# Dividing the third attention's products instead of its weights, an earlier spread of the inverses, and three of eight squares summed on GpSimd

## Chip, cores and metric

One NeuronCore of a Trainium2 chip runs the whole kernel. The metric is the device time of one execution in microseconds; three runs of the kernel before took 2602.8, 2603.32 and 2605.36, median 2603.32.

## What is computed

Two transformer blocks, run one after the other on a batch of one with 512 positions and a width of 1024. The first has a sparse attention with an index (layer A), a perceptron, an attention with a forgetting gate (layer B), a second perceptron and a last norm; the second has a grouped-query attention with norms and rotations of queries and keys (layer C here), a perceptron, a gated unit (gMLP) and a last perceptron, with modulation from a condition vector. What the change touches, of the reference:

```python
def rms_norm(x, g):
    x32 = x.astype(jnp.float32)
    y = x32 * lax.rsqrt(jnp.mean(x32 * x32, axis=-1, keepdims=True) + EPS)
    return (y * g.astype(jnp.float32)).astype(x.dtype)
...
    def one_block(q_blk):
        s = jnp.einsum('bqkgd,bskd->bkgqs', q_blk, k).astype(jnp.float32) * scale
        p = jax.nn.softmax(s, axis=-1).astype(v.dtype)
        return jnp.einsum('bkgqs,bskd->bqkgd', p, v)
```

The sum of squares of a norm runs over the width; the softmax of a head divides each row of weights by its sum, and dividing the product with v by the same sum gives the same result.

## The kernel before

Activations lie feature-major in eight tiles `h[k]` of 128x512 float32 (128 features by 512 positions). Precision comes from splitting each operand into a high and a low part (`split`, `weight`: high by a copy on ACT, low by a subtraction on DVE or GpSimd, names ending in h and l), and each product is three matmuls (`mul3`: high by high, low by high, high by low).

All instructions are recorded first and ordered afterwards by the program's own scheduler (`Sched`, from L155). `record` notes dependences and gives an instruction its place in the program as priority, plus what `later(n)` adds; `order` plays the engines with a table of costs and takes, on each engine that is free, the ready instruction of the lowest number whose output tile can be had; `emit` writes that order out. So all instructions carry the line L414. A tile of a name (tag) can be had when the earlier tiles of that tag have been begun, in their order, and one of its buffers is free. The eight PSUM banks are a pool with four tags: mm, lg and tp may have three each, po two, and all share four beyond the first of each. A bank of po is what heads' products, the sum of squares and the spreads use.

`squares` (L583) sums the squares of the eight `h[k]`: ACT squares into tiles "sq" (one buffer) and "y" in turn, DVE adds into `acc`, and four matmuls with ones sum over the features. `rms` (L601) makes the inverse root of it, and `spread` lays it out over all partitions by four transposes into a po bank and an ACT copy y. `rms` runs four times: at the start of layer A, ahead of the first perceptron, at the start of layer B, and ahead of the second perceptron.

`heads` (L813) treats a pair of heads. For each, `softmax` makes logits (lg), takes the masked row minimum (pr, mn, one DVE instruction each for the four blocks), exponentiates on ACT with the row sum beside it, and, unless `late` is set, makes a reciprocal (rs, 128x1) on DVE and scales pr by it on GpSimd. `turned` then transposes pr (tp), splits it into th and tl, and PE multiplies by v into a po bank; ACT copies one half (top) and DVE adds the other into `both` (o). With `late`, the sums of both heads are inverted together: `inverses` makes one reciprocal of 128x8, a wide copy on ACT (its tile is also called top, with one buffer) and four transposes into a po bank, and DVE multiplies `both` by that. Layer A calls `heads` with `late` 16 times (eight over half the positions, with the `narrow` form, eight over the other half); layer B and layer C call it eight times each without.

`layer_c` (L1066) also holds the first block's last norm: `spread(x.r)` and eight multiplications of `h` by its result (h<-h,vec,y) are recorded ahead of the attention under `later(2000)`, so that they give way to it. Then come the eight pairs, whose queries are projected, normed and rotated two pairs ahead (q, rot, sqh, msh, rh).

Of the kernel before, what the change touches and what calls it, by code (L numbers as in the profile page):

```python
# [14 lines left out]
ALU = mybir.AluOpType  # L15
# [3 lines left out]
P = 128  # L19
S = 512  # L20
# [3 lines left out]
NB = S // P  # L24
# [466 lines left out]
class Net:  # L491
# [91 lines left out]
    def squares(self, col=None):  # L583

        nc = self.nc
        acc = self.t(self.np_, "acc", [P, S])
        for k in range(KD):
            kw = {} if col is None else {"scale": self.vec[:, col + k : col + k + 1]}
            sq = acc if k == 0 else self.t(self.np_, "sq", [P, S], bufs=1) if k % 2 else self.t(self.np_, "y", [P, S])
            nc.scalar.activation(sq, self.h[k], AF.Square, **kw)  # L590
            if k:
                nc.vector.tensor_tensor(acc, acc, sq, ALU.add)
        ps = self.po()
        for b in range(NB):
            nc.tensor.matmul(ps[:, 2 * b : 2 * b + 2], acc[:, b * P : (b + 1) * P], self.ones[:, 0:2], start=True, stop=True)
        return ps[:, 0 : 2 * NB : 2]
# [216 lines left out]
    def heads(self, pool, npr, nth, lhs, rhs, v, o, masks=None, causal=True, rows=(None, None), blocks=range(NB), narrow=False, late=False):  # L813


        nc = self.nc
        n = len(blocks) * P
        W = {i: (i + 1) * P if causal else S for i in blocks}
        keys = range(max(W.values()) // P)
        sums = self.t(pool, "sums", [P, 2 * len(blocks)])  # L820
        both = self.t(pool, "o", [P, n], bufs=1)
        for h in range(2):
            pr = self.softmax(pool, npr, lhs[h], rhs[h], W, masks, rows[h], sums, h, late)
            po = self.po()
            for b in keys:
                th, tl, c = self.turned(pool, nth, pr, W, b)
                if narrow:
                    for x, (part, y) in enumerate(((0, th), (0, tl), (64, th))):
                        nc.tensor.matmul(po[0:64, c], v[h][b][:, part : part + 64], y[:, c], start=b == 0 and x == 0, stop=b == keys[-1] and x == 2)
                else:  # L830
                    nc.tensor.matmul(po[:, c], v[h][b], th[:, c], start=b == 0, stop=False)
                    nc.tensor.matmul(po[:, c], v[h][b], tl[:, c], start=False, stop=b == keys[-1])
            r = slice(64 * h, 64 * h + 64)
            if narrow:
                nc.scalar.activation(both[r], po[0:64, :n], AF.Copy)
            else:
                top = self.t(pool, "top", [P, n], bufs=1)[0:64]
                nc.scalar.activation(top, po[0:64, :n], AF.Copy)
                nc.vector.tensor_tensor(both[r], po[64:128, :n], top, ALU.add)
        if late:  # L840
            nc.vector.tensor_tensor(both, self.inverses(pool, sums, len(blocks)), both, ALU.mult)
        self.split(o[0][:, :n], o[1][:, :n], both)

    def attn_out(self, o, w, gate=None, norm=None):
# [221 lines left out]
    def layer_c(self, x, gate, norm):  # L1066
        nc, I, tc = self.nc, self.I, self.tc
        xh, xl = x.xh, x.xl
        *kps, q0 = self.first([I["w_k_c"][0], I["w_k_c"][1], I["w_q_c"][0]], xh, xl)
        with self.sched.after(), self.sched.later(2000):  # L1070
            rb = self.spread(x.r)
            for k in range(KD):
                g = self.vec[:, V_GF + k : V_GF + k + 1]
                nc.vector.scalar_tensor_tensor(self.h[k], self.h[k], g, rb, ALU.mult, ALU.mult)
        with ExitStack() as c1:
            pool = c1.enter_context(tc.tile_pool(name="c", bufs=2))
            tab = {}
            for w, col in (("q", V_QG), ("k", V_KG)):
                for m in range(2):
                    a = self.t(pool, f"tab{w}{m}", [P, S], bufs=1)  # L1080
                    nc.sync.dma_start(a, I["rope_c"][m])
                    nc.gpsimd.tensor_scalar(a, a, self.vec[:, col + m : col + m + 1], 1.0, ALU.mult, ALU.mult)
                    tab[w, m] = a
            v = [self.t(pool, f"v{b}", [P, 4, P], F32R, 1) for b in range(NB)]
            bd = self.t(pool, "bd", [P, 2], bufs=1)
            zero = self.t(pool, "zero", [P, S], bufs=1)
            nc.gpsimd.memset(zero, 0.0)
            nc.gpsimd.memset(bd, 0.0)
            nc.gpsimd.memset(bd[0:64, 0:1], 1.0)
            nc.gpsimd.memset(bd[64:128, 1:2], 1.0)  # L1090

            def inverse(ps, st):

                sq = self.t(pool, "sqh", [P, S], bufs=1)
                nc.scalar.activation(sq, ps, AF.Square)
                for b in range(NB):
                    nc.tensor.matmul(st[:, 2 * b : 2 * b + 2], sq[:, b * P : (b + 1) * P], bd, start=True, stop=True)
                ms = self.t(pool, "msh", [P, 8])
                nc.vector.tensor_scalar(ms, st[:, 0:8], 1.0 / HD, EPS, ALU.mult, ALU.add)
                rr = self.t(pool, "rh", [P, 8], bufs=4)  # L1100
                nc.gpsimd.tensor_tensor(rr, ms, self.mhalf, ALU.pow)
                return rr

            def evac_v(b, ps):
                x = ps.rearrange("p (n d) -> p n d", n=4)
                self.split(v[b][:, :, 0:64], v[b][:, :, 64:128], x)

            kd = []
            self.tm(I["w_v_c"], xh, xl, evac_v, ("po", "po", "lg", "tp"))
            for ps in kps:  # L1110
                s = self.rope(pool, ps, tab["k", 0], tab["k", 1], nc.gpsimd)
                st = self.lg()
                rr = inverse(ps, st)
                wide = self.t(pool, "o", [P, S], bufs=1)
                nc.scalar.activation(wide.rearrange("p (a d) -> p a d", a=8), rr.rearrange("p (a o) -> p a o", o=1).to_broadcast([P, 8, HD]), AF.Copy)
                for b in range(NB):
                    nc.tensor.transpose(st[:, b * P : (b + 1) * P], wide[:, b * P : (b + 1) * P], self.ident)
                nc.vector.tensor_tensor(s, st, s, ALU.mult)
                kd += self.doubles(pool, "kd", s, -0.125)
            qs, o = [], []  # L1120
            for j in range(KD + 2):
                if j < KD:
                    with self.sched.later(200 if j > 1 else 0):
                        self.low = nc.gpsimd if j > 2 else None
                        ps = q0 if j == 0 else self.fm(I["w_q_c"][j], xh, xl)
                        self.low = None
                        s = self.rope(pool, ps, tab["q", 0], tab["q", 1], nc.gpsimd if j else nc.vector)
                        rr = inverse(ps, ps)
                        qs.append((self.stacks(pool, "st", s, 16), rr))
                if j < 2:  # L1130
                    continue
                j -= 2
                st, rr = qs[j]
                n = j // 2
                o.append(self.two(pool, "st", 16))
                self.heads(pool, 3, 2, [(q, q) for q in st], [kd[n]] * 2, [[x[:, n, :] for x in v]] * 2, o[j], [zero] * NB, causal=False,
                           rows=[[rr[:, 2 * b + h : 2 * b + h + 1] for b in range(NB)] for h in range(2)])
            self.attn_out(o, I["w_o_c"], gate, norm)

# [303 lines left out]
```

## Time and profile before

| | |
|---|---|
| median of 3 runs | 2603.32 us (2602.8 to 2605.36) |
| the profiled execution | 2607.56 us |
| its span | 2605.5 us |
| PE, weight loads (PEld) busy | 2547.2 us (98%), 2162.3 us (83%) |
| DVE, ACT, GpSimd busy | 1579.6 (61%), 1172.7 (45%), 389.7 us (15%) |

The span is the time between the first and the last instruction of the profile. PE's busy time counts overlapping pipelined matmuls up to their modelled ends, so 98% does not mean that PE works at its full rate all the time. Names are those of the program, with the numbers of the buffers left out.

### The profile page before, as it was taken

Reading aid. Unit: us, or ns where it says so; the run is one execution under the profiler, and the core shown is the slowest. Engines: PE = TensorE matmul, PEld = TensorE weight load, DVE = VectorE, ACT = ScalarE, POOL = GpSimd, SP = SyncE. Lnnn points to the kernel's source line nnn. Section 1 sums busy time; section 2 is a strip of 40 time slices with the busy share of each in tenths; the row PEclk is TensorE's granted clock in tenths of the full one; section 3 lists DMA queues with packets and bytes.
Section 4 is the critical chain, followed back from the end, with each engine's and each line's share of the span. In section 5 each row is a group of like instructions: output and inputs, shape, how many; then the busy total and the mean of one; then the engine's idle time right before and its main releaser. Section 6 shows DMA issues by size and latency. Waiting matters only on the chain.

```text
span 2605.5 us, 34328 instructions
## 1 busy us (share of the span) xinstructions
PE 2547.2 (98%) x12966; PEld 2162.3 (83%) x12966; DVE 1579.6 (61%) x2699; ACT 1172.7 (45%) x2116; POOL 389.7 (15%) x389
## 2 busy tenths in 40 slices
PE   7989999999999999999989999999999999999999
PEld 6779788888988878888867888888998888888887
DVE  7998865645488766646798634435447654634433
ACT  5677322334498423334776523323336443523322
POOL 4740000000063000002664200001002110200000
PEclk9999999999999999999999999999999999999999
DMA  4322755423221656522210222222333332322222
GB/s 155 89 64 85 255 195 177 139 96 114 89 62 58 221 183 199 164 97 98 77 44 26 98 97 97 97 97 93 93 108 124 101 95 91 96 96 96 96 97 95
DMA packets 90837, 290.32 MB, mean 111 GB/s; under 512 B 11536, under 2 KB 15888, under 8 KB 90672
## 3 DMA queue, kind: packets, MB, share of 16 engines
q1 hardware_dynamic: 90672, 288.14, 34.5%
q8 instruction: 101, 1.65, 0.3%
q14 instruction: 64, 0.52, 0.1%
HBM read 277.28 MB, written 2.10 MB: 107 GB/s over the span
## 4 chain that ended last, share of the span: by engine, by line
PE 81%; DVE 9%; ACT 4%; DMA 3%; issue 2%; POOL 0%; SPq 0%; DVEq 0%; ACTq 0%; POOLq 0%
PE mm L414 70%; PE lg L414 4%; PE tp L414 4%; PE po L414 3%; DMA adaw<-in_ada_w 3%; DVE st L414 1%; DVE mask L414 1%; DVE tl L414 1%; DVE ada L414 1%; ACT pr L414 1%; DVE pr L414 1%; DVE acc L414 1%; DVE o L414 0%; ACT wh L414 0%; DVE m L414 0%
## 5 line engine op out<-in xcount | busy, mean ns | idle before, releaser
L414 ACT ACTIVATE wh<-wr 128x1024 fp32r<-128x1024 f32 (+2 forms) x480 | 449.2, 942 | 1067.9 <-PE mm L414 920.8
L414 DVE TENSOR_TENSOR wl<-wr,wh 128x1024 fp32r<-128x1024 f32 (+1 forms) x382 | 453.0, 1186 | 306.3 <-ACT wh L414 300.0
L414 PE MATMUL mm<-xh,wh 128*128 128x512 f32 (+1 forms) x1640 | 623.9, 381 | 8.9 <-ACT wh L414 8.9
L414 PE MATMUL mm<-xl,wh 128*128 128x512 f32 (+1 forms) x1640 | 623.6, 381 | 0.7 <-POOL xl L414 0.4
L414 PE MATMUL mm<-xh,wl 128*128 128x512 f32 (+1 forms) x1640 | 623.3, 380 | 0.6 <-POOL wl L414 0.6
L414 PE MATMUL mm<-ah,wh 128*128 128x512 f32 (+1 forms) x1072 | 408.8, 381 | 3.3 <-ACT ah L414 3.3
L414 PE MATMUL mm<-al,wh 128*128 128x512 f32 (+1 forms) x1072 | 408.4, 381 | 0.5 <-DVE al L414 0.4
L414 PE MATMUL mm<-ah,wl 128*128 128x512 f32 (+1 forms) x1072 | 407.6, 380 | 0.0
L414 PEld LDWEIGHTS mm<-xh,wh 128*128 128x128 f32 x1640 | 310.1, 189 | 62.7 <-ACT wh L414 9.3
L414 PEld LDWEIGHTS mm<-xh,wl 128*128 128x128 f32 x1640 | 310.5, 189 | 56.3 <-POOL wl L414 1.0
L414 PEld LDWEIGHTS mm<-xl,wh 128*128 128x128 f32 x1640 | 310.5, 189 | 54.9 <-POOL xl L414 1.3
L414 PEld LDWEIGHTS mm<-ah,wh 128*128 128x128 f32 x1072 | 202.4, 189 | 42.3 <-ACT ah L414 4.2
L414 DVE SCALAR_TENSOR_TENSOR h<-mm,mod,h 128x512 f32<-128x512 f32 (+1 forms) x113 | 79.8, 707 | 260.0 <-PE mm L414 259.8
L414 PEld LDWEIGHTS mm<-al,wh 128*128 128x128 f32 x1072 | 202.2, 189 | 39.5 <-DVE al L414 1.6
L414 PEld LDWEIGHTS mm<-ah,wl 128*128 128x128 f32 x1072 | 202.2, 189 | 38.2
L414 POOL TENSOR_TENSOR wl<-wr,wh 128x512 fp32r<-128x512 f32 x98 | 134.8, 1386 | 197.0 <-ACT wh L414 191.2
L414 DVE TENSOR_TENSOR h<-mm,h 128x512 f32<-128x512 f32 (+1 forms) x91 | 56.6, 626 | 138.7 <-PE mm L414 138.7
L414 DVE SCALAR_TENSOR_TENSOR ada<-adaw,cs,ada 128x512 f32<-128x512 f32 x168 | 118.1, 748 | 34.6 <-DMA adaw<-in_ada_w 34.2
L414 ACT ACTIVATE pr<-pr,mn 128x128 f32<-128x128 f32 (+2 forms) x192 | 116.9, 612 | 13.9 <-DVE mn L414 13.4
L414 ACT ACTIVATE ah<-a 128x512 fp32r<-128x512 f32 x128 | 81.1, 634 | 83.7 <-DVE a L414 81.6
L414 PE MATMUL tp<-ident,pr 128*128 128x128 f32 x576 | 112.2, 279 | 6.6 <-DVE tl L414 3.5
L414 DVE TENSOR_TENSOR al<-a,ah 128x512 fp32r<-128x512 f32 x128 | 88.3, 692 | 45.8 <-ACT ah L414 45.8
(258 smaller groups left out, 3896.9 us busy)
## 6 DMA issues: line engine op xcount, KB each, us to landing
adaw<-in_ada_w SPq DMA_DIRECT2D x96, 512.0 KB
wr<-in_w_up SPq DMA_DIRECT2D x64, 512.0 KB
wr<-in_w_down SPq DMA_DIRECT2D x64, 512.0 KB
wr<-in_w_in SPq DMA_DIRECT2D x64, 512.0 KB
wr<-in_w_out SPq DMA_DIRECT2D x64, 512.0 KB
wr<-in_w_gu SPq DMA_DIRECT2D x24, 512.0 KB
wr<-in_w_gv SPq DMA_DIRECT2D x32, 384.0 KB
wr<-in_w_go SPq DMA_DIRECT2D x32, 384.0 KB
```

Of the source, the lines that this page charges most:

```text
L414: getattr(getattr(self.nc, o.eng), o.name)(*args, **kw)
```

## The change

`squares` puts the second square straight into a second tile `acc2` and has GpSimd add the fourth and sixth to it, while DVE adds the third, fifth, seventh and eighth to `acc`; DVE then adds the two. `heads` with `late` makes the inverses after the second head's weights are exponentiated and ahead of its products, where they stood behind both heads' products. Layer C's eight calls of `heads` become `late`.

```diff
@@ squares
-        acc = self.t(self.np_, "acc", [P, S])
+
+        acc, acc2 = self.t(self.np_, "acc", [P, S]), self.t(self.np_, "acc", [P, S])
         for k in range(KD):
             kw = {} if col is None else {"scale": self.vec[:, col + k : col + k + 1]}
-            sq = acc if k == 0 else self.t(self.np_, "sq", [P, S], bufs=1) if k % 2 else self.t(self.np_, "y", [P, S])
+            a, eng, tag = (acc2, nc.gpsimd, "sq") if k in (1, 3, 5) else (acc, nc.vector, "y")
+            sq = a if k < 2 else self.t(self.np_, tag, [P, S], bufs=1 if tag == "sq" else None)
             nc.scalar.activation(sq, self.h[k], AF.Square, **kw)
-            if k:
-                nc.vector.tensor_tensor(acc, acc, sq, ALU.add)
+            if k > 1:
+                eng.tensor_tensor(a, a, sq, ALU.add)
+        nc.vector.tensor_tensor(acc, acc, acc2, ALU.add)
@@ heads
             pr = self.softmax(pool, npr, lhs[h], rhs[h], W, masks, rows[h], sums, h, late)
+            if late and h:
+                inv = self.inverses(pool, sums, len(blocks))
             po = self.po()
...
         if late:
-            nc.vector.tensor_tensor(both, self.inverses(pool, sums, len(blocks)), both, ALU.mult)
+            nc.vector.tensor_tensor(both, inv, both, ALU.mult)
@@ layer_c
-                self.heads(pool, 3, 2, [(q, q) for q in st], [kd[n]] * 2, [[x[:, n, :] for x in v]] * 2, o[j], [zero] * NB, causal=False,
+                self.heads(pool, 3, 2, [(q, q) for q in st], [kd[n]] * 2, [[x[:, n, :] for x in v]] * 2, o[j], [zero] * NB, causal=False, late=True,
```

How this moves instructions, at three places. First GpSimd at the start of layer A, behind its first memsets; before (acc and sq are the sums and squares, wl the low parts of weights, r the inverse root):

```order
10 L414 ISA
11 L414 TENSOR_TENSOR wl_194<-wr_113,wh_186 128x512 x2
12 L414 TENSOR_TENSOR wl_248<-wr_140,wh_240 128x512
13 L414 TENSOR_TENSOR r_259<-ms_253,mhalf_84 128x4
14 L414 TENSOR_TENSOR wl_248<-wr_140,wh_240 128x512
```

and in the change:

```order
10 L414 ISA
11 L414 TENSOR_TENSOR acc_168<-acc_168,sq_181 128x512
12 L414 TENSOR_TENSOR wl_204<-wr_113,wh_197 128x512
13 L414 TENSOR_TENSOR acc_168<-acc_168,sq_202 128x512
14 L414 TENSOR_TENSOR wl_204<-wr_113,wh_197 128x512
15 L414 TENSOR_TENSOR wl_248<-wr_140,wh_232 128x512
16 L414 TENSOR_TENSOR r_259<-ms_245,mhalf_84 128x4
```

The two additions come in front of the two halves of the first weight's subtraction. Then PE in layer C, at the end of the first pair's first head and the beginning of its second; before (po are the products of a head, po_12554 the first and po_12650 the second, lg logits, tp transposes of weights):

```order
6286 L414 MATMUL po_12554<-tl_12599,v_2664_12269 128x512
6287 L414 MATMUL tp_12618<-ident_105,pr_12462 128x128 x4
6288 L414 MATMUL lg_12596<-kdl_12375,st_12455 128x512
6289 L414 MATMUL mm_12347<-bd_12021,sqh_12614 128x2 x2
6290 L414 MATMUL tp_12628<-ident_105,pr_12462 128x128 x4
6291 L414 MATMUL mm_12347<-bd_12021,sqh_12614 128x2 x2
6292 L414 MATMUL mm_12437<-xl_2586_11895,wh_12279 128x512
6293 L414 MATMUL mm_12437<-xh_2578_11875,wl_12292 128x512
6294 L414 MATMUL lg_12643<-kdh_12359,st_12466 128x512
6295 L414 MATMUL lg_12643<-kdl_12375,st_12466 128x512
6296 L414 MATMUL po_12650<-th_12605,v_2661_12193 128x512
```

and in the change, where the first head's products are po_12513 and end in row 6282, the inverse's four transposes are row 6300, and po_12117 is the spread of the last norm and po_12790 the second head's products:

```order
6348 L414 MATMUL mm_12668<-xh_2580_11917,wl_12384 128x512
6349 L414 MATMUL po_12117<-ident_105,rf_11739 128x128 x3
6350 L414 MATMUL lg_12757<-kdh_12377,st_12709 128x512
6351 L414 MATMUL lg_12757<-kdl_12386,st_12709 128x512
6352 L414 MATMUL lg_12761<-kdh_12377,st_12709 128x512
6353 L414 MATMUL lg_12761<-kdl_12386,st_12709 128x512
6354 L414 MATMUL mm_12668<-bd_12021,sqh_12770 128x2 x4
6355 L414 MATMUL mm_12788<-xh_2573_11779,wh_12641 128x512
6356 L414 MATMUL po_12790<-th_12556,v_2661_12193 128x512
```

The second head's products have moved from ten rows behind the first head's to 74 behind, and the last three transposes of the spread stand just ahead of them. Last DVE at the same place; before (tl are the low parts of turned weights, ISA with pr the masked minimum):

```order
1536 L414 TENSOR_TENSOR tl_12616<-tp_12582,th_12605 128x512
1537 L414 ISA pr_12529,mn_12530<-lg_12596,zero_12010,rh_12453 128x512
1538 L414 ISA mn_12530 128x1
1539 L414 TENSOR_TENSOR o_12640<-po_12554,top_12623 64x512
1540 L414 TENSOR_TENSOR tl_12648<-tp_12603,th_12630 128x512
1541 L414 RECIPROCAL rs_12656<-sums_12551 128x1
1542 L414 TENSOR_SCALAR msh_12658<-mm_12347 128x8
1543 L414 TENSOR_TENSOR q_12574<-q_12574,tabq_2657_11850 128x512
1544 L414 ISA pr_12673,mn_12674<-lg_12643,zero_12010,rh_12453 128x512
1545 L414 ISA mn_12674 128x1
1546 L414 TENSOR_TENSOR tl_12681<-tp_12618,th_12663 128x512
```

and in the change:

```order
1543 L414 ISA pr_12726,mn_12727<-lg_12738,zero_12010,rh_12633 128x512
1544 L414 ISA mn_12727 128x1
1545 L414 ISA pr_12726,mn_12727<-lg_12745,zero_12010,rh_12633 128x512
1546 L414 ISA mn_12727 128x1
1547 L414 TENSOR_SCALAR msh_12786<-mm_12668 128x8
1548 L414 SCALAR_TENSOR_TENSOR h_5_86<-h_5_86,vec_80,y_12784 128x512
1549 L414 SCALAR_TENSOR_TENSOR h_6_88<-h_6_88,vec_80,y_12784 128x512
1550 L414 TENSOR_TENSOR tl_12806<-tp_12575,th_12796 128x512
1551 L414 TENSOR_TENSOR tl_12811<-tp_12584,th_12802 128x512
1552 L414 SCALAR_TENSOR_TENSOR h_7_92<-h_7_92,vec_80,y_12784 128x512
1553 L414 TENSOR_TENSOR tl_12826<-tp_12609,th_12814 128x512
1554 L414 TENSOR_TENSOR q_12766<-q_12766,tabq_2657_11850 128x512
```

Masked minima and tl, which alternated, now stand apart: minima first, then the two multiplications that use the spread, then the tl of the second head. From row 1548 of the change to the end of layer C, DVE has 58 tl, 44 pr, 6 reciprocals, 15 additions o, 8 products with the inverse, 4 q and 8 st<-o.

## Rows read from the trace of the kernel before

**Rows 1.** Stretches: window, then busy us (instructions) of PE, PEld, DVE, ACT, POOL; clock; DMA.

```profile
65.00:130.00 65.00, 58.83 (x341) 48.33 (x341) 63.94 (x174) 44.78 (x111) 47.99 (x38) 1.00 0.30 88
1105.00:1170.00 65.00, 65.00 (x293) 53.92 (x292) 26.81 (x31) 17.75 (x22) 0.00 (x0) 1.00 0.30 97
1276.00:1396.00 120.00, 111.99 (x587) 87.27 (x586) 114.30 (x260) 96.29 (x211) 76.13 (x76) 0.99 0.14 43
```

**Rows 2.** DVE groups by shape, 1310.9 to 1432: count | busy us, mean ns | idle before, releasers.

```profile
L414 DVE TENSOR_TENSOR tl<-tp,th 128x512 fp32r<-128x512 f32 x52 | 34.5, 685 | 7.1 <-ACT th L414 6.4 <-PE po L414 0.3
L414 DVE CUSTOM_DVE_ANT_0 pr<-lg,zero,rh 128x512 f32<-128x512 f32 x46 | 33.7, 741 | 0.6 <-PE lg L414 0.4
L414 DVE TENSOR_TENSOR o<-po,top 64x512 f32<-64x512 f32 x14 | 9.7, 694 | 2.6 <-ACT top L414 2.1
L414 DVE TENSOR_TENSOR st<-q,st 64x512 fp32r<-64x512 f32 x10 | 9.0, 900 | 0.3
L414 DVE SCALAR_TENSOR_TENSOR h<-h,vec,y 128x512 f32<-128x512 f32 x8 | 7.6, 972 | 0.0
L414 DVE RECIPROCAL rs<-sums 128x1 f32<-128x1 f32 x48 | 6.9, 156 | 1.4 <-ACT pr L414 1.3
L414 DVE TENSOR_TENSOR q<-q,tabq 128x512 f32<-128x512 f32 x5 | 5.2, 1047 | 0.1
L414 DVE TENSOR_TENSOR st<-o,st 128x512 fp32r<-128x512 f32 x7 | 4.9, 693 | 0.9 <-ACT st L414 0.7
```

**Rows 3.** Timeline, start of layer A: start us, length us, instruction, [idle before <-releaser].

```profile
12.84 1.14 ACT L414 ACTIVATE y<-h 128x512 f32<-128x512 f32 x2
...
16.91 1.67 DVE L414 TENSOR_TENSOR acc<-acc,y 128x512 f32<-128x512 f32 x1
...
20.20 0.69 DVE L414 TENSOR_TENSOR acc<-acc,sq 128x512 f32<-128x512 f32 x1
...
15.04 2.98 POOL L414 TENSOR_TENSOR wl<-wr,wh 128x512 fp32r<-128x512 f32 x2 [13.84 <-ACT wh L414]
```

**Rows 4.** Timeline, second perceptron's start: sum over features on PE, first use of the spread.

```profile
870.16 0.95 PE L414 MATMUL po<-ones,acc 128*128 128x2 f32 x8
...
874.87 0.69 DVE L414 SCALAR_TENSOR_TENSOR t<-mm,y 128x512 f32<-128x512 f32 x1
```

**Rows 5.** GpSimd groups by shape, 1310.9 to 1432: the scalings.

```profile
L414 POOL TENSOR_SCALAR pr<-pr,rs 128x512 f32<-128x512 f32 x48 | 39.0, 819 | 46.2 <-DVE rs L414 42.3 <-ACT th L414 2.7 <-DVE msh L414 1.0
```

**Rows 6.** Timeline of DVE in layer C without gaps.

```profile
1390.78 0.69 DVE L414 TENSOR_TENSOR tl<-tp,th 128x512 fp32r<-128x512 f32 x1
1391.38 0.74 DVE L414 CUSTOM_DVE_ANT_0 pr<-lg,zero,rh 128x512 f32<-128x512 f32 x1
...
1392.05 0.16 DVE L414 RECIPROCAL rs<-sums 128x1 f32<-128x1 f32 x1
1392.12 0.74 DVE L414 CUSTOM_DVE_ANT_0 pr<-lg,zero,rh 128x512 f32<-128x512 f32 x1
```

**Rows 7.** Timeline: the last norm's spread, first transpose on PE and copy on ACT.

```profile
1251.22 0.27 PE L414 MATMUL po<-ident,rf 128*128 128x128 f32 x1
...
1317.02 0.61 ACT L414 ACTIVATE y<-po 128x512 f32<-128x512 f32 x1
```

**Rows 8.** Timeline of PE in layer C: narrow matmuls, and seven transposes in a row.

```profile
1280.13 1.05 PE L414 MATMUL mm<-bd,sqh 128*128 128x2 f32 x8 [0.56 <-ACT sqh L414]
...
1350.48 0.93 PE L414 MATMUL tp<-ident,pr 128*128 128x128 f32 x7
```

**Rows 9.** Timeline of GpSimd and DVE late in layer C.

```profile
1401.34 1.65 POOL L414 TENSOR_TENSOR rh<-msh,mhalf 128x8 f32<-128x8 f32 x1
...
1404.22 0.70 POOL L414 TENSOR_SCALAR pr<-pr,rs 128x512 f32<-128x512 f32 x1
...
1406.91 1.29 DVE L414 TENSOR_TENSOR tl<-tp,th 128x512 fp32r<-128x512 f32 x2 [3.65 <-ACT th L414]
```

**Rows 10.** Timeline: end of layer C's last pair on DVE, and PE behind it.

```profile
1430.00 0.70 DVE L414 TENSOR_TENSOR o<-po,top 64x512 f32<-64x512 f32 x1 [1.25 <-ACT top L414]
...
1431.42 2.04 PE L414 MATMUL mm<-st,wh 128*128 128x512 f32 x4 [2.07 <-ACT st L414]
```

## The prediction, made before the changed kernel had run

> **What bounds the kernel now.** I read a table of stretches first, because a busy share over the whole span mixes stages with different limits. At the start of the first attention, layer A, DVE is busy 63.94 of 65 us, and in a perceptron (1105 to 1170) PE is busy 65.00 of 65 while DVE has 26.81 [rows 1]. The third attention, layer C, from about 1262 to 1436, which the change edits most, is between these: in 120 us of it DVE is busy 114.30 and PE 111.99 [rows 1]. So a DVE saving can count at the start and in C, and cannot in front of a perceptron. The groups of DVE work by shape price C's work and show what its idle time waited for [rows 2]. Then come the timelines of the places that the change touches.
>
> The profiled execution took 2607.56 us (span 2605.5 and 2.06 around it), 4.24 above the median of the three runs, 2603.32. I sum against the profile and take off the same 4.24. A measurement of this kernel tells a change from none at about 0.2%, 5.2 us.
>
> **The squares, first place.** Of the eight squares' seven additions on DVE five stay, one of them new (it joins the two halves), and GpSimd does two. Before, the third and fourth square (k=2, 3) leave ACT at 12.84 + 1.14 = 13.98; one of DVE's additions is stretched from 0.69 to 1.67 us beside two GpSimd subtractions that take 2.98 together, and the last ends at 20.20 + 0.69 = 20.89 [rows 3]. After the change GpSimd alternates: addition, half of a weight subtraction, addition, as the order shows. It can begin behind the fourth square, near 14.1. With 1.49 for each (2.98/2, an estimate for the addition too, since no GpSimd addition of this form is in the trace) that is 15.6, 17.1, 18.6; the joining addition follows in 0.69 (undisturbed) to 1.67 (stretched), to 19.3 or 20.3. So it gains 0.6 to 1.6; I take the middle, 1.1, for DVE is the bound right behind it and passes it on [rows 1]: **-1.1**. The slowed additions are the part of this that I know least. The Trainium skill ("SBUF — State Buffer", section "Who interferes with whom") says that a DVE operation with two SBUF inputs contends with a GpSimd operation that reads SBUF, and that the shared port is an exclusive lock. By that the joining addition waits for the subtraction behind the last GpSimd addition, to about 20.1, and ends at 20.8: a gain of 0.1. The stretched row above agrees in kind, though its excess of 0.98 is less than a whole operation of 1.49.
>
> **The other three places.** In front of both first-block perceptrons and layer B the sum is hidden: the matmul on it is issued at 870.16 with PE full of matmuls before and behind it, and the result is first used at 874.87 [rows 4]. The joining addition puts one more 0.69 on that path; two more banks of matmuls (24 at 65.00/293 = 0.222, 5.3 us [rows 1]) stand between, so I take 0. With the cover gone it is 3 x 0.69 = 2.1, and the bounds are 0 and 2.1: **0**.
>
> **Layer A's late pairs** divided their products already; the inverse only comes a head earlier. It is the same reciprocal, wide copy and transposes, so **0**; one turn of a bank (a copy of 0.61 as in rows 7 and an addition of 0.69 as in rows 2) more or less at the end bounds it by 1.3 either way.
>
> **Layer C, what goes and comes.** For each of eight pairs DVE loses eight reciprocals of 128x1 and GpSimd eight scalings (48 of the 64 lie behind 1310.9: 39.0 us at 819 ns) [rows 5]; DVE gains one wide reciprocal and one product of 128x512 with a PSUM operand, ACT one wide copy, PE four transposes. On DVE a reciprocal costs 0.07 from start to start (1392.05 to 1392.12), a PSUM operation 0.60 (1390.78 to 1391.38), a masked reduction (pr) 0.67 (1391.38 to 1392.05) [rows 6]. So per pair 0.56 goes and about 0.67 comes: no saving in DVE work itself. What can be gained is waiting.
>
> (a) **The bank.** `spread(x.r)` for the final norm was recorded under later(2000). Its first transpose runs at 1251.22, its result is only copied at 1317.02: for 66 us it holds one of the two po banks [rows 7]. Before, heads take the other in turn. After, the first pair's inverse takes that other bank and keeps it until the division, which needs the second head's products, which need a bank too. So the second head cannot begin until the spread ends. In the order, PE's three remaining transposes of it stand just ahead of the second head's products; in the order of before the second head began ten rows after the first ended. From 1280.13, the same place in both orders, to row 6348 of the change PE has 87 matmuls of 512 columns (0.222), 40 transposes (seven in 0.93 less the end of the last, so 0.11) and the narrow ones (1.05) [rows 8]: 24.8 us, and at the busy share 111.99/120 [rows 1] 26.5, so the spread ends near 1307. ACT has a square and a weight's copy ahead of its own copy, which I put at its end between 1309 and 1311; I take 1310.9. By then DVE has done the 20 masked reductions (five heads) that buffers allow, and waits. From there to the end it has, against the rows of before from 1310.9 on [rows 2]: 58 tl for 52, 44 pr for 46, 6 reciprocals for 48, 15 o for 14, 8 products for none, 4 q for 5, 8 st<-o for 7. At the starts' distances (and 1.0 for q): +3.6 -1.3 -2.9 +0.6 +4.8 -1.0 +0.6 = **+4.3**.
>
> (b) **Contention.** DVE operations with two SBUF inputs run long next to GpSimd: st<-q takes 900 ns, h 972 and q 1047, where those with a PSUM operand take 685 to 694 [rows 2]. Against 0.69, 10 st<-q, 8 h and 5 q have 2.1 + 2.3 + 1.8 = 6.2 too much. GpSimd was busy 76.13 of 120 us [rows 1], and 48 scalings in 121 us are 39.0 [rows 5], so about half of its work goes: **-3.0**, bounds 0 and -4.5, since what stays is longer work, as rh's 1.65 and its successor [rows 9].
>
> (c) **The queue.** From 1401.34 rh and, behind it, rot stand in front of a scaling at 1404.22, whose weights then have to be transposed and copied; DVE idles 3.65 us to 1406.91 [rows 9]. Without the scaling the chain does not pass GpSimd: **-3.65**.
>
> (d) **Reciprocals** wait in DVE's order for ACT's exponentials, 1.3 us of 1.4 idle [rows 2]: **-1.3**.
>
> (e) **Bank bubbles.** Each later pair now needs a third bank turn. The evacuations o wait 2.6 us over 14 [rows 2], 0.19 each; for 8 divisions **+1.5**. The bounds are 0 and 7 x 1.3 = 9.1, where each later pair waits for the copy (0.61) and addition (0.69) that free its bank. I take the low end, for DVE and PE have other heads' work to fill with.
>
> (f) **The tail.** The last head's addition starts at 1430.00, and PE goes on at 1431.42 after waiting 2.07 [rows 10]. The last division stands in that path: **+0.7**, as one o.
>
> C comes to 4.3 - 3.0 - 3.65 - 1.3 + 1.5 + 0.7 = -1.45, and all to -1.1 + 0 + 0 - 1.45 = -2.55: 2607.56 - 2.55 = 2605.0 on the profile's scale, 2600.8 as a median.
>
> **Rivals.** *Faster*: the stall is made up and DVE's waits behind 1310.9 go, except for the tail. They are 7.1 + 2.6 + 1.4 = 11.1 [rows 2], of which I leave 2.8 for the tail's path (PE's wait of 2.07 and one o [rows 10]). Then 4.3 - 3.0 - 8.3 - 1.1 = -8.1, 2595.2. For it: most wait for ACT's th, behind GpSimd's scalings. Against it: the two banks. 0.30.
>
> *Slower*: the bank turn decides. Each of seven later pairs cannot start its products until the earlier pair's second head has been copied and added, 1.3 each, 9.1. The wait at 1404 is then not got back, since another stands in its place: 4.3 + 9.1 - 3.0 - 1.3 - 1.1 = +8.0, 2611.3. It decides from the point where DVE has no masked reductions left while it waits. The Trainium skill ("Perfetto Trace Analysis", "Optimization Strategy") says that a gap which repeats on the engine that should be saturated can mean too little PSUM; no run here shows yet that this is such a case. For it: the stall at the spread is of this kind. Against it: before, o waited only 2.6 us in all. 0.24.
>
> *The change does not do what it says*: the additions move but none is on a path and C only trades waits, 2603. 0.03, no change.
>
> **How the numbers follow.** The forecast has 0.43. With the last rival that makes no change 0.46, faster 0.30, slower 0.24. The range reaches from the faster rival with contention at its bound (2595.2 - 1.3, to 2594) to the slower with a little of the squares' +2.1, 2612. The forecast's own range is 2598 to 2605.
>
> **What would show it.** In the changed profile the last addition into acc should end between 19 and 20.8. In C the spread's copy y should end near 1311 with DVE idle ahead of it for at least the 4.3 us that it falls behind; GpSimd should have no scalings; st<-q should fall below 900 ns. I am wrong if DVE does not stand still ahead of y, if o waits over 5 us in all, or if layer A's end moves by more than 2 us either way.

## The result, and the profile after

The changed kernel takes 2616.49 us (median of 5 runs, 2611.16 to 2620.75) where the one before, run beside it, takes 2602.8. The ratio is 1.0054, 95% interval 1.0037 to 1.0071: 10 to 18 us slower. The forecast was 2600.8 and its range ended at 2612. The profiled execution took 2614.97, 7.4 us more than the one before; both are off their medians, in opposite directions.

Where the time went shows when the same instruction of both traces is compared. The sum over features of the first norm comes at the same time (-0.1 us), the first mask of layer A 4.3 us later, layer A's 16 heads of the first half begin 7 to 11 us later, its last outputs 10 us later. In the second perceptron 3 us come back, by a stretch at half clock that only the trace of before has (910 to 930, granted clock 0.86 to 0.97). Layer C adds 0.4 us, and the norm behind it 1.5 (the granted clock there, 1472 to 1482, is 0.83). So the loss is in layer A, where I had put -1.1 and 0.

The stretches of [rows 1] in the changed kernel, and two of layer A behind them (columns as there):

```profile
65.00:130.00 65.00, 59.95 (x328) 50.05 (x326) 63.63 (x159) 40.50 (x95) 45.38 (x37) 0.95 0.32 95
1105.00:1170.00 65.00, 65.00 (x293) 53.87 (x291) 26.60 (x30) 17.02 (x20) 0.00 (x0) 1.00 0.30 100
1276.00:1396.00 120.00, 114.91 (x612) 90.26 (x611) 104.99 (x213) 99.07 (x214) 40.22 (x28) 0.99 0.15 45
20.00:30.00 10.00, 8.77 (x38) 7.08 (x39) 3.24 (x7) 2.12 (x4) 5.89 (x6) 0.83 0.28 78
175.00:190.00 15.00, 7.97 (x41) 6.35 (x41) 14.40 (x41) 8.44 (x23) 6.20 (x5) 0.77 0.21 70
```

Before, the stretch 20 to 30 reads:

```profile
20.00:30.00 10.00, 8.66 (x45) 7.16 (x46) 5.17 (x11) 3.90 (x8) 6.57 (x5) 1.00 0.52 149
```

The granted clock was 1.00 there and is 0.83 now, 0.95 from 65 to 130 (before 1.00) and 0.77 from 175 to 190 (before 0.89). In layer C GpSimd's work has fallen from 76.13 to 40.22 us, about half, as forecast. DVE's fell from 114.30 to 104.99, though no DVE work was forecast to go: the window now holds more of its waiting.

The start of layer A, on GpSimd, DVE and PE (start us, length us, instruction, idle before):

```profile
13.86 1.29 POOL L414 TENSOR_TENSOR acc<-acc,sq 128x512 f32<-128x512 f32 x1 [12.66 <-ACT sq L414]
15.42 1.42 POOL L414 TENSOR_TENSOR wl<-wr,wh 128x512 fp32r<-128x512 f32 x1 [0.26 <-ACT wh L414]
16.80 1.74 POOL L414 TENSOR_TENSOR acc<-acc,sq 128x512 f32<-128x512 f32 x1
18.69 3.21 POOL L414 TENSOR_TENSOR wl<-wr,wh 128x512 fp32r<-128x512 f32 x2
...
14.34 4.76 DVE L414 TENSOR_TENSOR acc<-acc,y 128x512 f32<-128x512 f32 x3 [0.35 <-ACT y L414]
19.20 1.58 DVE L414 TENSOR_TENSOR acc<-acc,acc 128x512 f32<-128x512 f32 x1
...
20.83 1.05 PE L414 MATMUL po<-ones,acc 128*128 128x2 f32 x8 [1.36 <-DVE acc L414]
...
22.76 0.58 PE L414 MATMUL mm<-xh,wh 128*128 128x512 f32 x1
23.14 0.63 PE L414 MATMUL mm<-xl,wh 128*128 128x512 f32 x1
...
26.40 0.60 PE L414 MATMUL po<-ident,r 128*128 128x128 f32 x4
...
27.38 0.23 DVE L414 TENSOR_SCALAR wi<-po,r 128x8 f32<-128x8 f32 x1 [5.30 <-PE po L414]
```

and at the same place before:

```profile
15.52 1.35 DVE L414 TENSOR_TENSOR acc<-acc,sq 128x512 f32<-128x512 f32 x1 [0.85 <-ACT sq L414]
...
20.95 1.05 PE L414 MATMUL po<-ones,acc 128*128 128x2 f32 x8 [1.10 <-DVE acc L414]
...
25.47 0.23 DVE L414 TENSOR_SCALAR wi<-po,r 128x8 f32<-128x8 f32 x1 [3.26 <-PE po L414]
...
26.42 0.69 DVE L414 TENSOR_TENSOR cos<-cos,y 128x512 f32<-128x512 f32 x1
27.02 1.79 DVE L414 TENSOR_TENSOR sin<-sin,y 128x512 f32<-128x512 f32 x1
```

Where the two subtractions followed each other from 15.04 to 18.02 [rows 3], the second half of the first weight now starts at 18.69. The joining addition ends at 20.78, 0.11 earlier than before: not 0.6 to 1.6, but what the exclusive lock of the Trainium skill ("SBUF — State Buffer", "Who interferes with whom") gave, 0.1. Here that rule and the trace agree. DVE's own additions add to it: four of the five run stretched (4.76 us for three, then 1.58), where before two of seven did (1.35, and 1.67 in [rows 3]). Then PE, whose ready matmuls have run out, waits 1.36 us (1.10 before), and behind 22.76 its matmuls take 0.63 us instead of 0.39: the lower of its two levels, 1.2 GHz. The spread of the norm, which stands behind them, runs at 26.40, and `wi`, the first use of the norm's factor, at 27.38; before it was 25.47.

In layer C the stall came as worked out, 6 to 8 us later since the kernel arrives later:

```profile
1286.01 1.05 PE L414 MATMUL mm<-bd,sqh 128*128 128x2 f32 x8 [0.55 <-ACT sqh L414]
...
1313.87 0.49 PE L414 MATMUL po<-ident,rf 128*128 128x128 f32 x3
...
1318.07 0.58 ACT L414 ACTIVATE y<-po 128x512 f32<-128x512 f32 x1
...
1318.85 0.17 DVE L414 TENSOR_SCALAR msh<-mm 128x8 f32<-128x8 f32 x1 [3.05 <-ACT y L414]
```

From the narrow matmuls (1280.13 in [rows 8]) the spread is 27.9 us away, where 26.5 was forecast. DVE stands still for 3.05 us just ahead of `msh`, and for 7.3 us in all from 1305 on. DVE's groups from there on (1318.7 to 1440) answer to [rows 2]:

```profile
L414 DVE TENSOR_TENSOR tl<-tp,th 128x512 fp32r<-128x512 f32 x58 | 38.5, 686 | 5.4 <-ACT th L414 4.0 <-PE po L414 0.9
L414 DVE CUSTOM_DVE_ANT_0 pr<-lg,zero,rh 128x512 f32<-128x512 f32 x44 | 31.3, 743 | 0.1
L414 DVE TENSOR_TENSOR o<-po,top 64x512 f32<-64x512 f32 x15 | 10.4, 694 | 2.0 <-ACT top L414 1.4
L414 DVE TENSOR_TENSOR st<-q,st 64x512 fp32r<-64x512 f32 x10 | 6.9, 686 | 2.9 <-ACT st L414 2.6
L414 DVE SCALAR_TENSOR_TENSOR h<-h,vec,y 128x512 f32<-128x512 f32 x8 | 6.4, 805 | 0.0
L414 DVE TENSOR_TENSOR o<-po,o 128x512 f32<-128x512 f32 x8 | 5.5, 684 | 0.0
L414 DVE TENSOR_TENSOR q<-q,tabq 128x512 f32<-128x512 f32 x4 | 3.3, 813 | 0.3 <-DMA rot<-q 0.3
L414 DVE RECIPROCAL rs<-sums 128x8 f32<-128x8 f32 x6 | 1.2, 195 | 0.9 <-ACT pr L414 0.9
```

The counts are those forecast (58, 44, 15, 8, 6, 4). st<-q fell from 900 to 686 ns, h from 972 to 805, q from 1047 to 813. The evacuations o wait 2.0 us in all, so the bank bubbles of the slower rival (9.1) did not come. Of the signs named ahead, the stall and the fall of st<-q came; the one that says the forecast is wrong came too: layer A's end moved by 10 us, where more than 2 was to count against it.

### The profile page after: what moved, and what is told of

Read it like the earlier page. It is cut to its first block, busy times and chain, and to the rows that moved or that the text cites. A ratio compares the mean times of both kernels' runs of the same rounds, so it can differ in the third digit from the quotient of the medians.

```text
span 2613.2 us, 34226 instructions
## 1 busy us (share of the span) xinstructions
PE 2556.9 (98%) x12998; PEld 2172.3 (83%) x12998; DVE 1579.6 (60%) x2643; ACT 1174.1 (45%) x2124; POOL 350.9 (13%) x333
## 3 DMA queue, kind: packets, MB, share of 16 engines
q8 instruction: 102, 1.67, 0.3%
```

## Experiments

The layer A loss can come from the squares or from the earlier inverses, and the traces of one execution do not separate them. All ratios below are against the kernel before on the same chip, with their 95% intervals; 0.001 is 2.6 us. Chips differ between groups of runs, so runs of different groups are compared by these ratios.

**The parts alone.** Only the new `squares`:

> Only the squares of the change. Theory: the loss is in layer A and the squares start it: the GpSimd additions delay a weight's low half, PE stands still a little longer ahead of the sum over features, its clock falls to half for some us at 22 to 27 us, and the delay of about 4 us at 37 us and 6 us at 65 us follows; the kernel is 6 to 10 us slower than before, with a granted clock below 0.95 in the stretch 22 to 65. Rival (the earlier inverses in layer A make most of it): 0 to +3 us. Rival of the prediction (the squares gain 1.1 at the start and pass it on): -1 us.

Measured: 1.0024 (1.0014 to 1.0034), 6 us slower, clock 0.83 at 20 to 30 us.

Only the inverses moved ahead, everything else as before:

```diff
             pr = self.softmax(pool, npr, lhs[h], rhs[h], W, masks, rows[h], sums, h, late)
+            if late and h:
+                inv = self.inverses(pool, sums, len(blocks))
```

> Only the earlier inverses, which without the layer C part touch layer A's 16 late calls alone. Theory (the squares make the loss): -2 to +2 us, layer A's end within 2 us of before. Rival (the earlier inverses hold a po bank through the second head's products and cost layer A the 4 us by which its delay grows between 100 and 245 us): +3 to +5 us, with PE's clock lower in 100 to 200 than before.

Measured: 1.0025 (1.0016 to 1.0035), also 6 us slower. The rival's side was right, a little above its range; but the clock from 100 to 200 is 0.98 as before, and the bank that it names is put to the test below.

Only `late=True` in layer C, the inverse at the end as before:

> Only layer C's division of products, with the inverses made behind both heads' products as before. Theory: layer C trades 64 short reciprocals and 64 scalings for 8 inverses and 8 products, and comes out within 2 us of before, -2 to +2. Rival (the bank that the spread of the last norm holds is what costs, and an inverse at the end needs no bank beside the second head's products): -4 to -8 us.

Measured: 0.9981 (0.9971 to 0.9991), 5 us faster than before.

Layer C as in the change, squares and layer A as before (`if late and h and not causal`):

> Layer C as in the change (division of products, inverse ahead of the second head's products), squares and layer A as before. Theory: layer C of the changed kernel shifted the rest by 0 to +1 us in the trace, so -1 to +2 us. Rival (layer C holds the loss and the shift in layer A is disturbance of that one execution): +8 to +14 us.

Measured: 1.0001 (0.9991 to 1.0012).

The whole change again:

> The whole change again, on the same chip as the others of this call. If the parts add up (squares +6.3, early inverses in layer A +6.5, layer C as changed +0.3) it is 11 to 15 us slower than before; if the squares and the early inverses hide each other's delay in layer A, 6 to 9.

Measured: 1.0054 (1.0040 to 1.0067). The three parts, 0.0024 + 0.0025 + 0.0001, make 0.0050. They add up.

**The squares.** At the first place only, GpSimd's additions go back to DVE, in two chains:

```diff
-            a, eng, tag = (acc2, nc.gpsimd, "sq") if k in (1, 3, 5) else (acc, nc.vector, "y")
+            a, eng, tag = (acc2, nc.vector if self.first_sum else nc.gpsimd, "sq") if k in (1, 3, 5) else (acc, nc.vector, "y")
```

> The squares alone as in the run before with squares only, but at their first place, the start of layer A, all additions stay on DVE in two chains; GpSimd adds at the other three places only. Theory (GpSimd's additions at the first place delay the weights' low halves, PE stands still and its clock falls): no half clock between 22 and 65 us, layer A within 2 us of before at 65 us, and in all -1 to +2 us against before. Rival (the other three places, or any other order at the start, cost the 6 us): +4 to +7.

Measured: 1.0004 (0.9992 to 1.0015). The loss is gone, so it needs GpSimd's additions at the first place, and the other three places cost nothing that shows. The clock was not at 1.00 throughout, as I had expected:

```profile
20.00:30.00 10.00, 9.61 (x49) 7.94 (x48) 4.95 (x10) 2.25 (x5) 5.69 (x6) 0.97 0.40 124
30.00:65.00 35.00, 31.35 (x138) 25.59 (x137) 27.32 (x34) 19.93 (x39) 16.37 (x11) 0.95 0.36 107
```

Its half clock came earlier (17 to 20 us, behind a wait of 1.03 for a weight's low half), ahead of the sum and not between the sum and its spread; `wi` ran at 24.75.

Then work for PE in the wait. Six matmuls recorded ahead of the norm:

> The squares of the change with GpSimd, and six extra matmuls of 512 columns, whose result nothing reads, recorded ahead of the first sum over features, so that PE has work while it waits. Theory (the wait lets the clock fall, and the half clock is about 2 of the 4 us by which the first use of the norm is late): granted clock 1.00 from 20 to 30 us and the delay at 40 us falls from 4.2 to 2 to 3 us; in all 2 to 4 us faster than squares alone, so +2 to +4 against before. Rival (the clock is a companion, the delay comes from DVE and GpSimd contending): the delay at 40 us stays at 4 or more, +6 to +8 in all.

Measured: 1.0014 (1.0005 to 1.0024). This test missed its aim: the matmuls ran at 14.79, ahead of the wait, which grew to 1.82 us, and the clock at 20 to 30 was 0.83, as without them. The delay at 40 us (by how much the mask instruction that runs at 40.05 before comes later) fell from 4.2, with the squares alone, to 3.2. So something beside that stretch of half clock can change the delay; in this order two of DVE's operations behind the norm, cos and sin, ran undisturbed (0.68 and 0.69 us instead of 1.77 each with the squares alone; before, 0.69 and 1.79). The second filler depends on GpSimd's sum and so falls into the wait:

```diff
+        if self.first_sum:
+            fill = self.lg()
+            for b in range(18):
+                nc.tensor.transpose(fill[:, b % 4 * P : (b % 4 + 1) * P], acc2[:, b % 4 * P : (b % 4 + 1) * P], self.ident)
         nc.vector.tensor_tensor(acc, acc, acc2, ALU.add)
```

> The squares of the change, and 18 extra transposes of GpSimd's finished half sum, whose result nothing reads, so that PE works between the end of that sum and the first sum over features, where it stood still for 1.38 us; the six matmuls tried before ran ahead of the wait and left it 1.82 us long. Theory (the wait lets the clock fall): PE's wait ahead of the sum is under 0.7 us, the granted clock is 1.00 from 20 to 30 us, the first use of the norm's factor (wi) comes at 25.5 to 26 instead of 27.3, and the delay at 40 us is 2 to 3 us. Rival (the clock falls for another reason, as the activity ahead of it): clock 0.83 there as before and the delay at 40 us is 4 or more.

Measured: 1.0015 (1.0006 to 1.0024). Stretches and timeline of this kernel:

```profile
20.00:30.00 10.00, 9.56 (x54) 7.85 (x53) 5.96 (x10) 2.24 (x4) 7.43 (x6) 1.00 0.39 121
30.00:65.00 35.00, 29.85 (x137) 24.31 (x137) 29.31 (x34) 19.79 (x39) 14.24 (x10) 1.00 0.36 105
...
18.87 2.19 PE L414 MATMUL lg<-ident,acc 128*128 128x128 f32 x18
21.10 1.05 PE L414 MATMUL po<-ones,acc 128*128 128x2 f32 x8
...
24.93 0.23 DVE L414 TENSOR_SCALAR wi<-po,r 128x8 f32<-128x8 f32 x1 [2.58 <-PE po L414]
...
25.89 1.72 DVE L414 TENSOR_TENSOR cos<-cos,y 128x512 f32<-128x512 f32 x1
27.54 1.77 DVE L414 TENSOR_TENSOR sin<-sin,y 128x512 f32<-128x512 f32 x1
```

PE no longer waits, the clock is 1.00 to 65 us, `wi` comes 2.4 us earlier than with the squares alone (27.30) and the delay at 40 us is 2.5 instead of 4.2. So the clock's fall at this place hangs on PE's wait; filling it brings back 2.4 us at `wi`, of which 1.7 are left at 40 us. What is left of the delay fits contention: between `wi` and 38 us five of DVE's operations with two SBUF inputs take 1.66 to 1.80 us instead of 0.69 (cos, sin and three more), where before two do (1.79 each). Three more at about 1.05 us are 3.1, less the 0.5 by which `wi` is ahead of before. No run takes this contention away by itself. In all, 1.0015 against 1.0024 points the same way, but the two intervals overlap, and the filler that missed came out alike; so what the clock costs the whole kernel is not shown.

**The inverses.** First guess: an inverse holds one of two po banks through the second head's products. In layer A, all inverses in an lg bank:

> The earlier inverses in layer A as in the run with these alone (6.5 us slower than before), but all inverses take their bank from lg, which may have three, so that po keeps its two for the heads' products. Theory (the inverse holds one of two po banks through the second head's products): the loss goes, -2 to +2 us against before. Rival (the earlier place itself, a copy and four transposes ahead of the second head's work, costs): +4 to +7.

Measured: 1.0053 (1.0039 to 1.0066), worse than in po. Layer C's in an lg bank:

> Layer C's division with the early inverse (same time as before, where the inverse at the end was 5 us faster), its inverse in a bank of lg. Theory (po bank): as fast as with the inverse at the end or faster, -4 to -7 us against before. Rival (the early place or the missing logits bank costs as much): -1 to +2.

Measured: 1.0001 (0.9992 to 1.0010), as with po. In layer C, the bank that the last norm's spread holds is given back early (`spread(x.r)` out of `later(2000)`), with the early inverse and with that at the end:

> Layer C as in the change (early inverse), squares and layer A as before, but the last norm's spread is not put off: its four transposes run at once and give its po bank back near 1252. Theory (the spread's bank makes the early inverse's stall of the first pair's second head): 4 to 6 us faster than the early inverse in layer C alone, so -4 to -6 against before. Rival (each pair's inverse holds one of the two banks through the second head's products, whatever the spread does): no faster than that run, 0 to +2 against before.

> Layer C's division with the inverse at the end, and the spread not put off. Theory (a free second bank helps this order little, since the inverse never waited for the spread's bank with a head behind it): within 2 us of the run with the division at the end alone, -3 to -7 against before. Rival (with both banks free layer C runs without waits): -8 to -12.

Measured: 0.9997 (0.9987 to 1.0006) and 0.9980 (0.9971 to 0.9989). The stall is gone from the first one's trace (the second head's products start 4 us behind the first's, where 22.7 us lay between), and from the first product of layer C to the last it takes 139.7 us instead of 144.1. Yet by the medians it is only 1 us faster than with the stall, 5 faster to 3 slower. The end is 4 to 5 us better than the early place with or without the spread's bank.

Second guess: the order in which a tag hands out its banks. mm instead of po, early in layer A, early in layer C, and at the end in layer C:

> The earlier inverses in layer A alone (6.5 us slower than before with their bank in po, 13.8 with it in lg, whose turn the next head's logits then have to wait for), now with the bank in mm, whose next user is a projection or an output product and not the pair's own second head. Theory (a bank is handed out in the order of recording, so the second head's products cannot begin before the inverse has, and the inverse needs the last exponential, a reciprocal and a wide copy): -2 to +3 us against before. Rival (the early copy and transposes themselves, or one bank less in all, cost it): +4 to +8.

> Layer C's division with the early inverse (0.3 us slower than before with its bank in po or in lg), now with the bank in mm. Theory (turn in po or lg): as fast as with the inverse at the end, -3 to -7 against before. Rival (one bank less in all, or the early work itself): -1 to +2.

> Layer C's division with the inverse at the end and the spread not put off (5.2 us faster than before), with the inverse's bank in mm, so that the next pair's products need not wait for the inverse to begin. Theory (turn in po): -6 to -10 against before. Rival (at the end the turn costs nothing, since the next head is not ready earlier): within 2 us of that run, -3 to -7.

Measured: 1.0419 (1.0402 to 1.0437), 1.0030 (1.0018 to 1.0043) and 1.0046 (1.0034 to 1.0058). All three are worse. Tiles of a tag begin in the order in which they were recorded, so the projections recorded behind an inverse had to wait for it; that this is the reason is read from the program and not from a trace. It shows what a turn can cost (109 us), and it does not show that the turn in po is the cause; as tests of that, these three failed.

Where in layer A: early inverses in the second eight calls alone.

> The earlier inverses in the second eight of layer A's sixteen late calls alone. If the loss comes where PE and DVE have little else to do, at the end of layer A (the last two pairs' products ended 9 us later in the trace of all sixteen): +4 to +7 against before. If it comes from the first eight, whose products lie among other work: -2 to +2.

Measured: 1.0031 (1.0021 to 1.0041). The loss is in the second eight. The first eight, of the narrow form, copy a head's products straight into `both` and use no tile `top`. In layer A a call has two of the four blocks, so its inverse is a copy of 128x256 and two transposes. In the trace of the kernel with all early inverses, one pair there reads (ACT, DVE and PE; the first head's last product ends at 205.0):

```profile
205.28 0.36 ACT L414 ACTIVATE top<-po 64x256 f32<-64x256 f32 x1
...
206.06 0.43 DVE L414 TENSOR_TENSOR o<-po,top 64x256 f32<-64x256 f32 x1
...
206.85 0.41 ACT L414 ACTIVATE top<-rs 128x256 f32<-128x256 f32 x1
...
207.71 0.38 PE L414 MATMUL po<-ident,top 128*128 128x128 f32 x2
208.16 0.31 PE L414 MATMUL po<-th,v 128*128 128x256 f32 x1
```

The wide copy of the reciprocals is a tile `top` as the evacuations are, and `top` has one buffer. So it waits for the first head's products, their copy and their addition; the inverse waits for it, and the second head's products wait for the inverse, which is ahead of them in po: 3.1 us between the heads. Over the last eight pairs of layer A, the mean time from the end of one head's products to the start of the next is 0.3 us within a pair and 2.5 between pairs before, and 3.1 and 1.3 here: 1.6 us more for each pair. The last test gives the wide copy a tile of its own:

```diff
-        wide = self.t(pool, "top", [P, m * HD], bufs=1)
+        wide = self.t(pool, "wide", [P, m * HD], bufs=1)
```

> The earlier inverses in layer A alone (6.5 us slower than before), with a tile of their own for the wide copy, which otherwise shares the one buffer of top with the evacuations of both heads. Theory (the wide copy has to wait until the first head's products are done, copied to top and added, and the second head's products wait in their turn for the inverse: the two heads of a pair, whose products ran without a gap, are strung behind one another with 2 to 4 us between): most of the loss goes, -2 to +2 us against before, and the gap between the two heads' products in the second eight pairs falls under 1.5 us. Rival (one po bank taken for the pair's second half is enough): +4 to +8.

Measured: 0.9985 (0.9975 to 0.9994): the 6 us are gone, and 4 more. In its trace (PE) the inverse no longer waits for the evacuation; it runs before the first head's last two products, and the second head begins at 205.35:

```profile
201.27 0.28 PE L414 MATMUL po<-tl,v 128*128 128x256 f32 x1
201.50 0.38 PE L414 MATMUL po<-ident,wide 128*128 128x128 f32 x2
202.38 0.22 PE L414 MATMUL po<-th,v 128*128 128x128 f32 x1
203.39 0.31 PE L414 MATMUL po<-tl,v 128*128 128x128 f32 x1
205.35 0.28 PE L414 MATMUL po<-th,v 128*128 128x256 f32 x1
```

The gaps are 1.7 within and 1.4 between pairs, 3.1 together as against 4.4 with the shared buffer and 2.8 before (within a pair a little over the 1.5 expected). So the shared buffer made the loss in layer A. The gain beyond that is not explained by these gaps: layer A's last products end at 233.1, before at 235.1, and the next perceptron adds to it. A buffer of its own with the inverse left at the end was not run by itself.

In layer C the copy went into the squares' buffer:

> Layer C's division with the early inverse and the spread not put off (0.8 us faster than before), with the wide copy in the buffer of the squares, which layer C does not use. Theory (the shared buffer strings the heads of a pair): 3 to 5 us faster than that, -4 to -6 against before, as with the inverse at the end. Rival (the po bank): -2 to +1.

Measured: 1.0005 (0.9996 to 1.0014). By the number the rival holds. But the edit reaches further than layer C: layer A's inverses, still at their end, write the squares' buffer too, and its trace comes out of layer A 2 us later than before. In layer C it takes 137.8 us from the first product to the last, between the 139.7 of the shared buffer and the 136.1 of the inverse at the end. So a part for the shared buffer in layer C is neither shown nor excluded.

## Why the prediction was wrong, point by point

- **The squares, first place (-1.1): wrong, and the step that failed is "DVE is the bound right behind it and passes it on".** Alone they cost 6 us. The gain to be passed on was mis-sized too: the sum came 0.11 earlier, not 1.1. I had stretched the joining addition alone, and read one stretched addition before where there were two; of the five now on DVE four are stretched. What I left out is whose queue the additions stand in: they put off the weight's second low half, PE ran dry for 1.36 us instead of 1.10, and its clock fell to the lower level just ahead of the norm's spread. I had listed GpSimd's order and read it only for the sum. The shown parts are that GpSimd's additions at this place make the loss and that filling PE's wait brings back 2.4 us of the delay at its spot; that the low half makes PE run dry is read from the order.
- **The other three places (0): right** as far as -2 to +4 us tells, in the run that leaves only these to GpSimd.
- **Layer A's late pairs (0, at most 1.3 either way): wrong.** They cost 6 us. The step was "the inverse only comes a head earlier. It is the same reciprocal, wide copy and transposes". The work is the same, its place in two queues of tiles is not: it now stands between the two evacuations in `top` and ahead of the second head in po. The first is what cost: with a buffer of its own the loss goes, the bank still in po. I had worked out the po half of this for layer C, and did not apply it to layer A, whose calls take the same code.
- **Layer C (-1.45): within what was measured,** 1.0001 for that part alone, or -2 to +3 us. Its steps: the stall's place (a) came out 1.4 us long of the forecast; contention (b) gave back 2.1 on st<-q, 1.3 on h and 0.9 on q (4 x 0.234), together 4.4 where 3.0 was taken; no scaling stands in GpSimd's queue (c) any more, but DVE's waits ahead of tl came to 5.4 instead of 7.1, so 1.7 came back and not 3.65; reciprocals (d) still wait 0.9 of 1.4; the bubbles (e) did not come in o, whose waits fell from 2.6 to 2.0, but 2.9 came on st<-q (0.3 before), which I had not listed; the tail (f) is 0.7 longer, as forecast (last o at 1436.89, PE on at 1439.03). Terms missed both ways by as much as their sum, so that the sum fits is luck in part.
- **The rivals.** The slower one gave the sign and 2611 us, by a mechanism that did not occur: o waited 2.0 us, not 9. The chance of slower, 0.24, was too low, because each of two moved pieces outside layer C had been set near nothing without a rival of its own.
- **Still open:** why in layer C the early place is 4 to 5 us behind the end. With the spread's bank given back early it stays 4 us behind; the shared buffer was not separated from layer A there; lg left it as it was, and mm changed other turns.

The end place in layer C without the rest, with the spread not put off (0.9980) or put off (0.9981), beats both kernels. The early inverse with its own tile in layer A (0.9985) does so too; the two together were not run.

## What to carry to other kernels

When an instruction moves, list every queue in which it has a place: its engine, but also each tile tag that hands out buffers in order of recording. A tile with one buffer shared by two uses strings those uses behind each other, and a buffer of its own was worth 10 us here, with the inverse at its early place. Where work goes to a second engine because the first is full, ask first what that engine was about to deliver, and whether TensorE is waiting for it.

## What was not expected of the hardware

A wait of 1.36 us on PE was followed, 0.9 us after the end of the eight narrow matmuls, by the lower clock for about 3.4 us; before, a wait of 1.39 us ahead of the matmul at 35.97 was followed by none (30 to 65: 1.00), and one of 1.10 ahead of the sum neither. So in these traces the length of one wait does not tell whether the clock falls. Over the whole span the granted clock was 0.992 in the changed kernel's profile and 0.995 before. With 18 transposes in the wait, it was 1.00 from 20 to 65.

In these traces DVE is not always the one that is held up beside GpSimd: before, cos took 0.69 us and the subtraction that starts beside it at 26.42 took 1.83 instead of 1.27, and sin behind it 1.79.
